# Expert numbers by steps, one-hots with pairs, modulation spread evenly, three projections by block

## The chip, the cores and the metric

One core of one Trainium2 chip runs the whole program. The metric is the device time of one execution in microseconds (us).

## The reference, cut to what matters

Two layers, each a mixer (HGRN2 and S5 branches, a merge and an output projection) and a PEER layer: a search for 16 of 16384 single-neuron experts per token and head, by two sets of 128 keys. The expert search is what the change rewrites:

```python
s = einsum('thpd,hpnd->thpn', q, keys)            # 8 heads, 2 halves, 128 keys
s1_v, s1_i = top_k(s[:, :, 0, :], 16)
s2_v, s2_i = top_k(s[:, :, 1, :], 16)
cand_v = s1_v[..., :, None] + s2_v[..., None, :]          # 16 x 16 sums
cand_i = s1_i[..., :, None] * 128 + s2_i[..., None, :]    # their expert numbers
top_v, top_j = top_k(cand_v, 16)
idx = take_along_axis(cand_i, top_j)
gate = softmax(top_v)
act = gelu(einsum('thkd,td->thk', u_tab[idx], h))
out = einsum('thk,thkd->td', gate * act, v_tab[idx])
```

The mixer starts with `mod = silu(c) @ ada_w[l] + ada_b[l]`, 48 vectors of 128 per layer, which scale, shift and gate the blocks of features.

## The kernel before

Everything is kept by blocks of 128 features (8) and 512 tokens. A dense matrix product is three matmuls per block, since both sides are split into a high and a low part (`whi`/`wlo` by ScalarE and VectorE, L114 and L116; the inputs are `ahi`/`alo`). Weights come in pieces of 128x1024 floats (512 KB), tile `raw`, four buffers, on SyncE's queue.

**Mixer.** Projections, eight heads, then gates, GLU and output projection. A modulation vector is one 128x1024 load, tile `ada`, and one multiply with a row sum on VectorE (L165). Between the gate projections, the GLU and the output products the code calls `later(n)`: 1 vector behind each of 8 projections, 3 ahead of each of 8 GLU products, 4 ahead of four output products.

**Expert stage.** 512 tokens are four blocks of 128. The last block's experts are gathered row by row with indirect DMAs (128 steps for U, L946 on VectorE; 128 for V, L957, tile `gr`, accumulator `gacc`). For the other 384 tokens the kernel computes all 16384 products of U: `dense_U`, 128 times 24 matmuls of 128x384, evicted as `uo` (L788) and written out to `sA`. The gates become a dense matrix by one-hot matmuls. `select(tb)` finds the experts of a token block: 16 best of 50 candidates per head by VectorE's maximum instructions, then, for each of 128 places, L855 compares a row of 50 counters with the found place and sums the candidates' expert numbers (tile `jk`). `build(tb, sel, g8)` makes for four tokens the one-hots of the two key numbers on VectorE (`P` L900, `Qo` L902), multiplies the second by the gate's high and low halves (`Q`, two times L906), and TensorE multiplies the pairs, eight f16 matmuls of 128x128 (L912, L913, tile `pa`). In `P` and `Q` the four tokens lie innermost, so that each matmul reads every fourth element. There are 96 builds per layer; the code puts one `dense_U` and one gather step behind every second. ScalarE evicts `pa` into `stg`, and 48 tokens at a time go out to `sW`.

**Value stage.** For each of 128 pieces of V, `A` (from `sA`) times `W` (from `sW`) on VectorE (L1007), a split into `gh`/`gl`, and 24 matmuls (L1020 to L1022) into eight accumulators that take all of PSUM.

The framework's scheduler orders each engine's instructions by priority and its own estimate of times, so the order within an engine is fixed when the program is built.

Of the kernel before, what the change touches and what calls it, by code (L numbers as in the profile page):

```python
# [4 lines left out]
F32 = mybir.dt.float32  # L5
# [11 lines left out]
T = 512  # L17
# [24 lines left out]
def trunk(tc, a, dbg=None, layers=L, n_i2=128):  # L42
# [17 lines left out]
    def ptile(shape, tag):  # L60
        return psp.tile(shape, F32, tag=tag, name=nm(tag), bufs=PB[tag])
# [420 lines left out]
    def mixer(l, h):  # L482
# [13 lines left out]
        G.memset(toe, 0.0)  # L496
        s5_maps(l, sm, fx, hp, ("w1", "w2", "w3"))
        pk0 = pack_tile(fx)
        dcol = fx.tile([128, 32], F32, name=nm("dcol"))
        for j in range(4):  # L500
            nc.sync.dma_start(dcol[32 * j:32 * j + 32, :], a["dsk"][l])
# [230 lines left out]
        gates(J - 2, fx)  # L732
# [5 lines left out]
        def later(n, l_=l, todo=todo):  # L738
            n = min(n, len(todo))
            if n:  # L740
                ada(l_, [todo.pop(0) for _ in range(n)], hp, "ada")

        for e in range(J):
            ps = proj(40 + e)
            sg = hp.tile([128, T], F32, tag="F", name=nm("sg"))
            S.activation(sg, ps, AF.Sigmoid)
            V.tensor_tensor(yap[:, e, :], yap[:, e, :], sg, op=OP.mult)
            later(1)
        ysf = fx.tile([128, J, T], F32, name=f"ysf{l}")
        ya = []  # L750
        for u in range(J):
# [6 lines left out]
        dump(f"ys{l}", ysf)  # L758
        mg = []
        for e in range(J):  # L760
            later(3)
            ps = dense(a["glu"][l, e], ya)
            sg = hp.tile([128, T], F32, tag="F", name=nm("sg"))
            S.activation(sg, ps, AF.Sigmoid, bias=vec["glub"][:, l, e:e + 1])
            V.tensor_tensor(sg, sg, sgb[e], op=OP.mult)
            V.tensor_tensor(yap[:, e, :], sg, yap[:, e, :], op=OP.add)
# [5 lines left out]
                                   op0=OP.mult, op1=OP.add)  # L772

        for e in range(J - 3):
            later(4, l + 1, follow)
# [22 lines left out]
    def peer(l, h, rows, gp):  # L798
# [13 lines left out]
        def scores(p, ps):  # L812
# [9 lines left out]
            for tb in range(NB):  # L822
                wk = rp.tile([128, 128], F32, tag="wk", name=nm("wk"))
                top16(sv[:, tb, p], sx[:, tb, p], s[:, tb], wk)

        def select(tb):
            val = sv[:, tb].rearrange("p (h s) k -> p h s k", s=2)
            idf = rp.tile([128, 16, 16], F32, tag="idf", name=nm("idf"), bufs=1)
            V.tensor_copy(idf, sx[:, tb])
            idv = idf[:].rearrange("p (h s) k -> p h s k", s=2)  # L830
            V.tensor_scalar(idv[:, :, 0, :], idv[:, :, 0, :], 128.0, None, op0=OP.mult)
            cv = rp.tile([128, 8, NCAND], F32, tag="cv", name=nm("cv"), bufs=1)
            ci = rp.tile([128, 8, NCAND], F32, tag="ci", name=nm("ci"), bufs=1)
            for src, dst in ((val, cv), (idv, ci)):
                for r in range(5):
                    n = CAND[r]
                    V.tensor_tensor(dst[:, :, COFF[r]:COFF[r] + n], src[:, :, 0, r:r + 1].to_broadcast([128, 8, n]),
                                    src[:, :, 1, 0:n], op=OP.add)
                V.tensor_tensor(dst[:, :, COFF[5]:COFF[8]].rearrange("p h (r b) -> p h r b", b=2),
                                src[:, :, 0, 5:8, None].to_broadcast([128, 8, 3, 2]),  # L840
                                src[:, :, 1, None, 0:2].to_broadcast([128, 8, 3, 2]), op=OP.add)
                V.tensor_tensor(dst[:, :, COFF[8]:], src[:, :, 0, 8:16],
                                src[:, :, 1, 0:1].to_broadcast([128, 8, 8]), op=OP.add)
            tv = rp.tile([128, 8, 16], F32, tag="tv", name=nm("tv"), bufs=1)
            tj = rp.tile([128, 8, 16], U32, tag="tj", name=nm("tj"), bufs=1)
            for hh in range(8):
                wk = rp.tile([128, NCAND], F32, tag="wk2", name=nm("wk2"))
                top16(tv[:, hh], tj[:, hh], cv[:, hh], wk)
            tf = rp.tile([128, 8, 16], F32, tag="tf", name=nm("tf"), bufs=1)
            V.tensor_copy(tf, tj)  # L850
            code = rp.tile([128, 8, 16], F32, tag="code", name=nm("code"), bufs=1)
# [5 lines left out]
            cint = rp.tile([128, 128], I32, tag="cint", name=nm("cint"), bufs=1)  # L857
            V.tensor_copy(cint, code[:].rearrange("p h k -> p (h k)"))
            ii = rp.tile([128, 2, 128], I32, tag="ii", name=nm("ii"), bufs=1)
            V.tensor_scalar(ii[:, 0], cint, 7, None, op0=OP.logical_shift_right)  # L860
            V.tensor_scalar(ii[:, 1], cint, 127, None, op0=OP.bitwise_and)
            fx = rp.tile([128, 3, 128], F32, tag="fx", name=nm("fx"), bufs=1)
            V.tensor_copy(fx[:, 0:2], ii)
# [15 lines left out]
            gh = rp.tile([128, 2, 128], F16, tag="gh", name=nm("gh"))  # L879
            V.tensor_copy(gh[:, 0], pt[:, 2])  # L880
            V.tensor_tensor(gh[:, 1], pt[:, 2], gh[:, 0], op=OP.subtract)
            return st, gh

        stg = {}
# [1 line left out]
        def build(tb, sel, g8):  # L886
# [7 lines left out]
            sh = [128, 128, NT]  # L894

            def row(t):
                return t[:, None, :].to_broadcast(sh)
# [5 lines left out]
            Qs = []  # L903
            for i in range(2):
                q = rp.tile(sh, F16, tag=f"Q{i}", name=nm("Q"))
                V.tensor_tensor(q, Q_, row(gh[:, i, c]), op=OP.mult)  # L906
                Qs.append(q)
            for b in range(NT // 4):
                ps = ptile([128, 4, 128], "pa")
                for k in range(4):  # L910
                    t = 4 * b + k
                    TE.matmul(ps[:, k], P_[:, :, t], Qs[0][:, :, t], start=True, stop=False)  # L912
                    TE.matmul(ps[:, k], P_[:, :, t], Qs[1][:, :, t], start=False, stop=True)  # L913
# [285 lines left out]
```

## Time and profile before

| | us |
|---|---|
| median of 3 runs | 3928.33 (3924.42 to 3931.42) |
| the profiled execution, its own time | 3930.45 |
| its span, first to last instruction | 3928.7 |
| TensorE busy in the span | 3736.3 (95%) |
| VectorE busy | 3238.6 (82%) |
| ScalarE busy | 1574.6 (40%) |
| GpSimd busy | 1021.7 (26%) |
| mean granted TensorE clock | 0.97 |

The profiled execution lies 0.05% above the median. Busy shares are means over stages: mixer, expert stage and value stage of each layer have different limits, so the stages are to be read apart.

### The profile page before, as it was taken

To read this page: it belongs to the slowest core of one execution; us is meant where nothing else is said; L and a number is where in the kernel's file an instruction comes from. 1 tells how busy PE (TensorE), PEld (TensorE's weight loads), DVE (VectorE), ACT (ScalarE), POOL (GpSimd) and SP (SyncE) were. 2 spreads that over 40 slices of the span, in tenths; PEclk is the share of its full clock that TensorE was granted. 3 is DMA by queue.
4 is the path that set the end of the run, shared out by engine and by line. 5 is a ranking of instruction groups with operands and counts; after the bars stand their busy time and mean duration, and the time that the engine had idled before them with its cause. 6 is when DMAs were issued, how large, how long until landed. Compare 5 with 4: busy or idle time off the path is not lost.

```text
span 3928.7 us, 62542 instructions
## 1 busy us (share of the span) xinstructions
PE 3736.3 (95%) x21878; PEld 3502.1 (89%) x21878; DVE 3238.6 (82%) x8715; ACT 1574.6 (40%) x2507; POOL 1021.7 (26%) x1475
## 2 busy tenths in 40 slices
PE   6999999999999959999999999999999997699998
PEld 5888878999999959999988887789999997699998
DVE  6998787999898879877578886679998888787874
ACT  3554443333343323333345554344333433233332
POOL 7454100013222344221033440000232223432210
PEclk9999999999999969999999999999999998899999
DMA  5222384379998989998622225524898898999984
GB/s 197 74 64 78 102 266 143 111 249 318 326 315 304 322 300 351 348 344 315 208 85 75 71 81 168 187 84 136 303 309 315 310 325 289 333 353 344 347 294 134
DMA packets 368764, 911.37 MB, mean 232 GB/s; under 512 B 35824, under 2 KB 187440, under 8 KB 368448
## 3 DMA queue, kind: packets, MB, share of 16 engines
q1 hardware_dynamic: 247696, 536.56, 40.6%
q0 software_dynamic: 73952, 268.56, 19.7%
q10 hardware_dynamic: 46800, 102.26, 6.8%
q8 instruction: 172, 2.82, 0.3%
q14 instruction: 144, 1.18, 0.1%
HBM read 796.09 MB, written 111.15 MB: 231 GB/s over the span
## 4 chain that ended last, share of the span: by engine, by line
PE 77%; DVE 11%; DMA 7%; POOL 2%; issue 2%; ACT 1%; SPq 0%; ACTq 0%; DVEq 0%; POOLq 0%
PE mm L132 12%; PE mm L133 12%; PE mm L134 12%; PE mm L1021 3%; PE mm L1020 3%; PE mm L1022 3%; PE pb L1021 2%; PE pa L1022 2%; PE pb L1020 2%; PE pa L1021 2%; PE pa L1020 2%; PE pb L1022 2%; DMA ada<-ada 2%; DVE wlo L116 2%; PE pa L912 2%; PE pa L913 2%
## 5 line engine op out<-in xcount | busy, mean ns | idle before, releaser
L114 ACT ACTIVATE whi<-raw 128x1024 fp32r<-128x1024 f32 x688 | 728.4, 1060 | 1289.0 <-PE mm L133 751.2
L133 PE MATMUL mm<-alo,whi 128*128 128x384 f32 (+1 forms) x3360 | 1217.2, 363 | 13.6 <-DVE alo L123 13.5
L134 PE MATMUL mm<-ahi,wlo 128*128 128x384 f32 (+1 forms) x3360 | 1216.7, 363 | 10.5 <-DVE wlo L116 10.4
L132 PE MATMUL mm<-ahi,whi 128*128 128x384 f32 (+1 forms) x3360 | 1216.7, 364 | 10.5 <-ACT ahi L229 3.5
L116 DVE TENSOR_TENSOR wlo<-raw,whi 128x1024 fp32r<-128x1024 f32 x688 | 842.1, 1225 | 319.6 <-ACT whi L114 299.5
L133 PEld LDWEIGHTS mm<-alo,whi 128*128 128x128 f32 x3360 | 638.0, 190 | 63.7 <-DVE alo L123 14.8
L134 PEld LDWEIGHTS mm<-ahi,wlo 128*128 128x128 f32 x3360 | 638.1, 190 | 62.6 <-DVE wlo L116 14.0
L132 PEld LDWEIGHTS mm<-ahi,whi 128*128 128x128 f32 x3360 | 638.5, 190 | 61.6 <-ACT ahi L229 4.6
L936 POOL DMA_INDIRECT gr<-ur,idi x256 | 269.5, 1053 | 1481.4 <-DVE jk L855 764.6
L936 POOL DMA_INDIRECT gr<-v,idi x256 | 350.6, 1370 | 669.1 <-DVE gacc L957 583.0
L957 DVE SCALAR_TENSOR_TENSOR gacc<-gr,gate,gacc 128x1024 f32<-128x1024 f32 x254 | 324.5, 1277 | 45.3 <-DMA gr<-v,idi 45.0
L946 DVE SCALAR_TENSOR_TENSOR gr<-gr,rows 128x1024 f32<-128x1024 f32 x256 | 311.1, 1217 | 25.9 <-DMA gr<-ur,idi 24.2
L1021 PE MATMUL mm<-gl,whi 128*128 128x384 f32 x768 | 259.0, 338 | 0.7 <-DVE gl L1011 0.6
L1022 PE MATMUL mm<-gh,wlo 128*128 128x384 f32 x768 | 258.5, 337 | 0.0
L1020 PE MATMUL mm<-gh,whi 128*128 128x384 f32 x768 | 210.0, 338 | 50.6 <-ACT gh L1009 26.4
L1009 ACT ACTIVATE gh<-A 128x384 fp32r<-128x384 f32 x256 | 132.4, 518 | 296.7 <-DVE A L1007 257.8
L912 PE MATMUL pa<-Q,P 128*128 128x128 f16 x768 | 197.7, 296 | 45.2 <-DVE Q L906 42.9
L855 DVE SCALAR_TENSOR_TENSOR jk<-iof,tf,ci 128x50 f32<-128x50 f32 x1024 | 223.8, 262 | 0.0
L914 ACT ACTIVATE stg<-pa 128x512 f32<-128x512 f32 x192 | 114.0, 598 | 220.4 <-PE pa L913 192.2
L913 PE MATMUL pa<-Q,P 128*128 128x128 f16 x768 | 187.9, 295 | 0.9
L1020 PEld LDWEIGHTS mm<-gh,whi 128*128 128x128 f32 x768 | 140.6, 189 | 51.2 <-ACT gh L1009 51.2
L1020 PE MATMUL pb<-gh,whi 128*128 128x384 f32 x512 | 172.8, 338 | 0.0
(382 smaller groups left out, 6642.9 us busy)
## 6 DMA issues: line engine op xcount, KB each, us to landing
raw<-u SPq DMA_DIRECT2D x256, 512.0 KB
raw<-v SPq DMA_DIRECT2D x256, 512.0 KB
raw<-win SPq DMA_DIRECT2D x112, 512.0 KB
ada<-ada SPq DMA_DIRECT2D x96, 512.0 KB
sA<-uo ACTq DMA_DIRECT2D x256, 192.0 KB
sW<-stg ACTq DMA_DIRECT2D x64, 768.0 KB
A<-sA SPq DMA_DIRECT2D x256, 192.0 KB
W<-sW SPq DMA_DIRECT2D x64, 768.0 KB
```

The source lines that it names most:

```text
L114: S.activation(hi, raw, AF.Copy)
L116: V.tensor_tensor(lo, raw, hi[:].bitcast(F32), op=OP.subtract)
L132: TE.matmul(ps, hi[:, w], ah, start=(j == 0), stop=False)
L133: TE.matmul(ps, hi[:, w], al, start=False, stop=False)
L134: TE.matmul(ps, lo[:, w], ah, start=False, stop=(j == J - 1))
L912: TE.matmul(ps[:, k], P_[:, :, t], Qs[0][:, :, t], start=True, stop=False)
L936: G.indirect_dma_start(out=g[:], out_offset=None, in_=tab, in_offset=bass.IndirectOffsetOnAxis(ap=ids[:, s_:s_ + 1], axis=0))
L946: V.scalar_tensor_tensor(g, g, 1.0, rows, op0=OP.mult, op1=OP.mult, accum_out=dot[:, s_:s_ + 1])
L957: V.scalar_tensor_tensor(acc_, g, gate[:, s_:s_ + 1], acc_, op0=OP.mult, op1=OP.add)
L1020: TE.matmul(ps, w[0][:, c], g[0], start=first, stop=False)
L1021: TE.matmul(ps, w[0][:, c], g[1], start=False, stop=False)
L1022: TE.matmul(ps, w[1][:, c], g[0], start=False, stop=last)
```

## The change

Four edits. In `select`, the expert number of a found place is no longer looked up among 50 candidates: `ranks` compares the place with 15 thresholds at once, adds up the differences between successive first-key numbers for the thresholds passed, and picks the second key among 16 by its rank, for half the heads at a time, in f16. In `build` both one-hots are made by one instruction, with the key numbers stored twice side by side, and each token's one-hot lies contiguous. The modulation vectors are spread evenly over 27 places from the gate projections to the output products, and those of the next layer join the list. The first layer's first three projections, whose weights are loaded at the start, are written as one loop over blocks of features.

```diff
+    thr = cst.tile([128, 15, 2], F16, name="thr")
...
+    def rank_tables():
+        V.tensor_copy(rnk, iof[:, 0:16, None].to_broadcast([128, 16, 2]))
+        for r in range(1, 16):
+            G.memset(thr[:, r - 1], float(COFF[r]))
+            G.memset(cnd[:, r - 1], float(CAND[r - 1]))
...
+            for j in range(J):
+                ah, al = h[j]
+                w = slice(128 * j, 128 * j + 128)
+                for i, (hi, lo) in zip(order, ws):
+                    TE.matmul(opened[i], hi[:, w], ah, start=(j == 0), stop=False)
+                    TE.matmul(opened[i], hi[:, w], al, start=False, stop=False)
+                    TE.matmul(opened[i], lo[:, w], ah, start=False, stop=(j == J - 1))
...
-        todo = list(range(16, 48))
-        follow = list(range(16)) if l + 1 < layers else []
+        todo = [(l, i) for i in range(16, 48)] + [(l + 1, i) for i in range(16) if l + 1 < layers]
+        parts = 6 + 8 + 8 + 5
+        share = [len(todo) * (k + 1) // parts - len(todo) * k // parts for k in range(parts)]
...
+        def ranks(iv, j, o0, o1):
+            j = j.rearrange("p h k -> p (h k)")
...
+            def total(w, n, o):
+                while n > 2:
+                    m = (n + 1) // 2
+                    V.tensor_tensor(w[:, 0:n - m], w[:, 0:n - m], w[:, m:n], op=OP.add)
+                    n = m
+                V.tensor_tensor(o, w[:, 0], w[:, 1], op=OP.add)
...
+            ge, w = work(15), work(15)
+            V.tensor_tensor(twos(ge), twos(j[:, None].to_broadcast([128, 15, 64])), pairs(thr, 15), op=OP.is_ge)
+            V.tensor_tensor(twos(w), twos(ge), pairs(cnd, 15), op=OP.mult)
+            r2 = rp.tile([128, 64], F16, tag="r2", name=nm("r2"), bufs=1)
+            total(w, 15, r2)
+            V.tensor_tensor(r2, j, r2, op=OP.subtract)
+            gate_rows(ge, step, 15)
+            total(ge, 15, o0)
+            o0 = o0.rearrange("p (h k) -> p h k", h=4)
+            V.tensor_tensor(o0, o0, iv[:, :, 0, 0:1].to_broadcast([128, 4, 16]), op=OP.add)
+            eq = work(16)
+            V.tensor_tensor(twos(eq), twos(r2[:, None].to_broadcast([128, 16, 64])), pairs(rnk, 16), op=OP.is_equal)
+            gate_rows(eq, second, 16)
+            total(eq, 16, o1)
...
-            for hh in range(8):
-                for k in range(16):
-                    jk = rp.tile([128, NCAND], F32, tag="jk", name=nm("jk"))
-                    V.scalar_tensor_tensor(jk, iof[:, 0:NCAND], tf[:, hh, k:k + 1], ci[:, hh], op0=OP.is_equal,
-                                           op1=OP.mult, accum_out=code[:, hh, k:k + 1])
...
-            st = rp.tile([128, 2, 128], F16, tag="slot", name=nm("slot"))
-            S.activation(st, pt[:, 0:2], AF.Copy)
...
+            st = rp.tile([128, 128, 2, 2], F16, tag="slot", name=nm("slot"), bufs=1)
+            gh = rp.tile([128, 128, 2, 2], F16, tag="gh", name=nm("gh"), bufs=1)
...
-            P_ = rp.tile(sh, F16, tag="P", name=nm("P"))
-            V.tensor_tensor(P_, io4, row(st[:, 0, c]), op=OP.is_equal)
-            Q_ = rp.tile(sh, F16, tag="Qo", name=nm("Qo"))
-            V.tensor_tensor(Q_, io4, row(st[:, 1, c]), op=OP.is_equal)
...
+            PQ = rp.tile([128, NT, 2, 128], F16, tag="PQ", name=nm("PQ"))
+            V.tensor_tensor(PQ[:].rearrange("p t i (a b) -> p (t i) a b", b=2), ioh[:, None].to_broadcast(sh), pairs(st),
+                            op=OP.is_equal)
...
-                    TE.matmul(ps[:, k], P_[:, :, t], Qs[0][:, :, t], start=True, stop=False)
+                    TE.matmul(ps[:, k], PQ[:, t, 0], QQ[:, t, 0], start=True, stop=False)
```

Where the instructions now stand. On TensorE, before, at the end of layer 0's expert stage (P and Q are the one-hots, the `mm` of L1020 is the first value accumulator), the last build ran straight into the value matmuls:

```order
L912 LDWEIGHTS P_12614
L912 MATMUL pa_12622<-Q_12618,P_12614 128x128
L913 LDWEIGHTS P_12614
L913 MATMUL pa_12622<-Q_12620,P_12614 128x128
L1020 MATMUL mm_15647<-gh_15666,whi_15657 128x384
L1020 MATMUL mm_15648<-gh_15666,whi_15657 128x384
L1020 MATMUL mm_15649<-gh_15666,whi_15657 128x384
```

In the changed kernel the last build of that layer (PQ, QQ) is followed by `dense_U` (`mm<-ahi,whi`):

```order
L982 LDWEIGHTS PQ_11522
L982 MATMUL pa_11527<-QQ_11524,PQ_11522 128x128
L983 LDWEIGHTS PQ_11522
L983 MATMUL pa_11527<-QQ_11524,PQ_11522 128x128
L142 MATMUL mm_13919<-ahi_6422,whi_13915 128x384
L143 MATMUL mm_13919<-alo_6423,whi_13915 128x384
L144 MATMUL mm_13919<-ahi_6422,wlo_13917 128x384
```

and the value matmuls (now L1090) follow on the last `dense_U`, 17 of them later:

```order
L143 MATMUL mm_14511<-alo_6435,whi_14507 128x384
L144 MATMUL mm_14511<-ahi_6434,wlo_14509 128x384
L142 MATMUL mm_14511<-ahi_6436,whi_14507 128x384
L143 MATMUL mm_14511<-alo_6437,whi_14507 128x384
L144 MATMUL mm_14511<-ahi_6436,wlo_14509 128x384
L1090 MATMUL mm_14552<-gh_14571,whi_14562 128x384
L1090 MATMUL mm_14553<-gh_14571,whi_14562 128x384
```

So 23 builds, counted on TensorE, that stood behind the last `dense_U` now stand before it. On VectorE, before, near the end of one look-up (`jk` into `code`, then the shifts that part the two keys, and the next block's candidate numbers `ci`):

```order
L116 TENSOR_TENSOR wlo_10220<-raw_10216,whi_10218 128x1024
L855 SCALAR_TENSOR_TENSOR jk_8045,code_7794<-iof,tf_7792,ci_7727 128x50
L855 SCALAR_TENSOR_TENSOR jk_8047,code_7794<-iof,tf_7792,ci_7727 128x50
L855 SCALAR_TENSOR_TENSOR jk_8049,code_7794<-iof,tf_7792,ci_7727 128x50
L858 CAST cint_8051<-code_7794 128x128
L837 TENSOR_TENSOR ci_8068<-idf_8064 128x8x16
L837 TENSOR_TENSOR ci_8068<-idf_8064 128x8x8
L837 TENSOR_TENSOR ci_8068<-idf_8064 128x8x5
L837 TENSOR_TENSOR ci_8068<-idf_8064 128x8x4
L860 TENSOR_SCALAR ii_8053<-cint_8051 128x128
L861 TENSOR_SCALAR ii_8053<-cint_8051 128x128
```

In the changed kernel, inside one `ranks` (`s` holds the comparisons, 960 = 15 x 64, halved by the sums; `gr` is a gather step):

```order
L126 TENSOR_TENSOR wlo_10189<-raw_10185,whi_10187 128x1024
L892 TENSOR_TENSOR s_9205<-s_9204,cnd 128x960
L874 TENSOR_TENSOR s_9205<-s_9205 128x448
L881 TENSOR_TENSOR s_9204<-s_9204,step_9200 128x960
L1016 SCALAR_TENSOR_TENSOR gr_9473,dot_8118<-gr_9473,rows_6421 128x1024
L874 TENSOR_TENSOR s_9205<-s_9205 128x256
L934 TENSOR_TENSOR fx_9199<-tv_9147 128x128
L126 TENSOR_TENSOR wlo_10257<-raw_10253,whi_10255 128x1024
L874 TENSOR_TENSOR s_9204<-s_9204 128x448
```

The 128 look-ups of a token block have become 40 longer instructions between the same splits and gather steps. The first step of the gathers stands behind 18 `dense_U` splits in layer 0 instead of 22, and 20 `gacc` steps instead of 26 stand before the first value product.

## Rows read from the trace of the kernel before

**Rows 1.** The page: busy time by engine, and the chain that ended last.
```profile
PE 3736.3 (95%) x21878; PEld 3502.1 (89%) x21878; DVE 3238.6 (82%) x8715; ACT 1574.6 (40%) x2507; POOL 1021.7 (26%) x1475
...
PE 77%; DVE 11%; DMA 7%; POOL 2%; issue 2%; ACT 1%; SPq 0%; ACTq 0%; DVEq 0%; POOLq 0%
```

**Rows 2.** Windows: each engine's busy us (instructions), granted clock, DMA share, GB/s.
```profile
757.00:840.00 83.00, 83.00 (x484) 83.00 (x483) 81.91 (x581) 35.52 (x50) 3.02 (x3) 1.00 0.56 171
840.00:1347.00 507.00, 504.74 (x3063) 490.24 (x3063) 460.68 (x1552) 198.12 (x291) 139.18 (x131) 1.00 0.91 318
1347.00:1436.00 89.00, 42.48 (x285) 35.15 (x283) 68.92 (x135) 21.66 (x37) 43.18 (x24) 0.61 0.83 292
1436.00:1860.00 424.00, 423.29 (x2394) 422.65 (x2394) 354.10 (x575) 153.33 (x199) 129.26 (x98) 0.99 0.95 341
2692.00:3373.00 681.00, 627.71 (x3817) 604.65 (x3815) 609.08 (x2255) 253.06 (x371) 179.25 (x158) 0.95 0.85 297
```

**Rows 3.** TensorE's waits, 757 to 1436 us: total, times, longest.
```profile
PE mm L1020 <- DMA s5s<-ldt: 24.2, 1, 24.2
PE pa L912 <- DVE Q L906: 20.8, 10, 7.0
```

**Rows 4.** The eviction of one candidate block, 757 to 1436 us: ns min/median/max, first, last.
```profile
L788 ACT ACTIVATE uo<-mm x128: 465/471/498, 757.1 to 1364.7; 128x384 f32<-128x384 f32 x128
```

**Rows 5.** Timeline of TensorE in that stage: start, us, line, names.
```profile
1060.21 0.33 PE L132 MATMUL mm<-ahi,whi 128*128 128x384 f32 x1
...
1063.33 0.33 PE L132 MATMUL mm<-ahi,whi 128*128 128x384 f32 x1
...
1063.68 0.29 PE L912 MATMUL pa<-Q,P 128*128 128x128 f16 x1
...
1064.75 0.43 PE L132 MATMUL mm<-ahi,whi 128*128 128x384 f32 x1
```

**Rows 6.** Timeline of TensorE in the first mixer, whole-width and 128-wide matmuls.
```profile
45.64 0.39 PE L134 MATMUL mm<-ahi,wlo 128*128 128x512 f32 x1
...
46.55 0.40 PE L134 MATMUL mm<-ahi,wlo 128*128 128x512 f32 x1
...
82.79 1.05 PE L627 MATMUL pa<-Q,K 128*128 128x128 f32 x8
...
83.68 1.06 PE L672 MATMUL pa<-R 128*128 128x128 f32 x8
```

**Rows 7.** VectorE's lines, 757 to 1436 us: count, busy us, mean ns, idle before.
```profile
L116 DVE TENSOR_TENSOR wlo<-raw,whi 128x1024 fp32r<-128x1024 f32 x128 | 156.3, 1221 | 26.0 <-ACT whi L114 25.5
...
L906 DVE TENSOR_TENSOR Q<-Qo,gh 128x512 f16<-128x512 f16 x192 | 73.0, 417 | 5.1 <-PE pa L912 5.1
...
L900 DVE TENSOR_TENSOR P<-io,slot 128x512 f16<-128x512 f16 x96 | 39.5, 416 | 5.8 <-PE pa L913 5.7
...
L1007 DVE TENSOR_TENSOR A<-A,W 128x384 f32<-128x384 f32 x2 | 1.0, 554 | 1.6 <-DMA W<-sW 1.6
```

**Rows 8.** Windows of the look-up's instructions alone (tile jk).
```profile
757.00:1436.00 679.00, 113.65 (x1024) 0.95 0.86 296
```

**Rows 9.** Timeline of the first hand-over to the value matmuls, all engines.
```profile
1427.45 0.33 SPq L1035 DMA_DIRECT2D A<-sA  x1
...
1427.83 0.43 SPq L1005 DMA_DIRECT2D W<-sW  x1
...
1434.45 1.03 DVE L1007 TENSOR_TENSOR A<-A,W 128x384 f32<-128x384 f32 x2 [1.63 <-DMA W<-sW]
...
1435.62 0.69 PE L1020 MATMUL mm<-gh,whi 128*128 128x384 f32 x1 [24.19 <-DMA s5s<-ldt]
```

**Rows 10.** TensorE's waits, 500 to 600 us and 2400 to 2540 us.
```profile
PE mm L133 <- DVE alo L123: 6.9, 2, 6.4
...
PE mm L133 <- DVE alo L123: 6.7, 1, 6.7
```

**Rows 11.** Timeline of GpSimd before the first layer's small S5 tables.
```profile
22.18 1.15 POOL L286 TENSOR_TENSOR s5s<-s5s 128x32 f32<-128x32 f32 x1 [15.16 <-DMA s5s<-are]
```

More of the change, by code (lines that the diff above doesn't have):

```diff
@@ L488, in mixer @@
         hp = hctx.enter_context(tc.tile_pool(name=f"hp{l}", bufs=2))
+        opened = {}
+        if l == 0:
+            order = list(pre)
+            ws = [pre.pop(i) for i in order]
+            for i in order:
+                opened[i] = ptile([128, T], "mm")
+            for j in range(J):
[5 more added lines that the diff above has]
+                    TE.matmul(opened[i], lo[:, w], ah, start=False, stop=(j == J - 1))
         def proj(i):
+            if i in opened:
+                return opened.pop(i)
             return dense(a["win"][l, i], h, w=pre.pop(i, None) if l == 0 else None)
@@ L498, in mixer @@
         pk0 = pack_tile(fx)
+        if l == 0:
+            rank_tables()
         dcol = fx.tile([128, 32], F32, name=nm("dcol"))
@@ L730, in mixer, with later @@
         hp = mctx.enter_context(tc.tile_pool(name=f"gp{l}", bufs=2))
-        gates(J - 2, fx)
         if l > 0:
             cond(fx, stp)
-        todo = list(range(16, 48))
-        follow = list(range(16)) if l + 1 < layers else []
[L738 to L741, printed above, removed]
+        todo = [(l, i) for i in range(16, 48)] + [(l + 1, i) for i in range(16) if l + 1 < layers]
+        parts = 6 + 8 + 8 + 5
+        share = [len(todo) * (k + 1) // parts - len(todo) * k // parts for k in range(parts)]
+        def later():
+            for _ in range(share.pop(0)):
+                l_, i = todo.pop(0)
+                ada(l_, [i], hp, "ada")
+        for _ in range(J - 2):
+            gates(1, fx)
+            later()
         for e in range(J):
@@ L760, in mixer @@
         for e in range(J):
-            later(3)
+            later()
             ps = dense(a["glu"][l, e], ya)
@@ L774, in mixer @@
         for e in range(J - 3):
-            later(4, l + 1, follow)
+            later()
             merge(e, dense(a["wout"][l, e], mg))
@@ L824, in scores, with work, pairs, twos @@
                 top16(sv[:, tb, p], sx[:, tb, p], s[:, tb], wk)
+        def ranks(iv, j, o0, o1):
+            j = j.rearrange("p h k -> p (h k)")
+            def work(n):
+                return rp.tile([128, T], F32, tag="s", name=nm("s"))[:].bitcast(F16)[:, 0:64 * n].rearrange(
+                    "p (r x) -> p r x", r=n)
+            def pairs(t, n):
+                return t[:, :, None, :].to_broadcast([128, n, 32, 2])
+            def twos(w):
+                return w.rearrange("p r (a b) -> p r a b", b=2)
+            def total(w, n, o):
[4 more added lines that the diff above has]
+                V.tensor_tensor(o, w[:, 0], w[:, 1], op=OP.add)
+            def gate_rows(w, t, n):
+                sh = [128, n * 4, 8, 2]
+                v = w.rearrange("p r (h a b) -> p (r h) a b", h=4, b=2)
+                V.tensor_tensor(v, v, t[:].rearrange("p r h b -> p (r h) b")[:, :, None, :].to_broadcast(sh), op=OP.mult)
+            step = rp.tile([128, 15, 4, 2], F16, tag="step", name=nm("step"), bufs=1)
+            two = [128, 4, 15, 2]
+            V.tensor_tensor(step[:].rearrange("p r h b -> p h r b"), iv[:, :, 0, 1:16, None].to_broadcast(two),
+                            iv[:, :, 0, 0:15, None].to_broadcast(two), op=OP.subtract)
+            second = rp.tile([128, 16, 4, 2], F16, tag="second", name=nm("second"), bufs=1)
+            S.activation(second[:].rearrange("p r h b -> p h r b"), iv[:, :, 1, :, None].to_broadcast([128, 4, 16, 2]),
+                         AF.Copy)
+            ge, w = work(15), work(15)
[12 more added lines that the diff above has]
+            total(eq, 16, o1)
@@ L834, in select @@
-            for src, dst in ((val, cv), (idv, ci)):
+            for src, dst in ((val, cv),):
                 for r in range(5):
@@ L848, in select @@
                 top16(tv[:, hh], tj[:, hh], cv[:, hh], wk)
-            tf = rp.tile([128, 8, 16], F32, tag="tf", name=nm("tf"), bufs=1)
-            V.tensor_copy(tf, tj)
-            code = rp.tile([128, 8, 16], F32, tag="code", name=nm("code"), bufs=1)
-            for hh in range(8):
-                for k in range(16):
-                    jk = rp.tile([128, NCAND], F32, tag="jk", name=nm("jk"))
-                    V.scalar_tensor_tensor(jk, iof[:, 0:NCAND], tf[:, hh, k:k + 1], ci[:, hh], op0=OP.is_equal,
-                                           op1=OP.mult, accum_out=code[:, hh, k:k + 1])
[L857 to L861, printed above, removed]
+            jf = rp.tile([128, 8, 16], F16, tag="jf", name=nm("jf"), bufs=1)
+            V.tensor_copy(jf, tj)
             fx = rp.tile([128, 3, 128], F32, tag="fx", name=nm("fx"), bufs=1)
-            V.tensor_copy(fx[:, 0:2], ii)
+            for hf in range(2):
+                ranks(idv[:, 4 * hf:4 * hf + 4], jf[:, 4 * hf:4 * hf + 4], fx[:, 0, 64 * hf:64 * hf + 64],
+                      fx[:, 1, 64 * hf:64 * hf + 64])
             gv = fx[:, 2].rearrange("p (h k) -> p h k", h=8)
@@ L876, in select @@
                 TE.transpose(pt[:, i], fx[:, i], ident)
-            st = rp.tile([128, 2, 128], F16, tag="slot", name=nm("slot"))
-            S.activation(st, pt[:, 0:2], AF.Copy)
-            gh = rp.tile([128, 2, 128], F16, tag="gh", name=nm("gh"))
-            V.tensor_copy(gh[:, 0], pt[:, 2])
-            V.tensor_tensor(gh[:, 1], pt[:, 2], gh[:, 0], op=OP.subtract)
+            st = rp.tile([128, 128, 2, 2], F16, tag="slot", name=nm("slot"), bufs=1)
+            gh = rp.tile([128, 128, 2, 2], F16, tag="gh", name=nm("gh"), bufs=1)
+            for i in range(2):
+                S.activation(st[:, :, i], pt[:, i, :, None].to_broadcast([128, 128, 2]), AF.Copy)
+            g2 = pt[:, 2, :, None].to_broadcast([128, 128, 2])
+            V.tensor_copy(gh[:, :, 0], g2)
+            V.tensor_tensor(gh[:, :, 1], g2, gh[:, :, 0], op=OP.subtract)
             return st, gh
@@ L911, in build @@
                     t = 4 * b + k
-                    TE.matmul(ps[:, k], P_[:, :, t], Qs[0][:, :, t], start=True, stop=False)
-                    TE.matmul(ps[:, k], P_[:, :, t], Qs[1][:, :, t], start=False, stop=True)
+                    TE.matmul(ps[:, k], PQ[:, t, 0], QQ[:, t, 0], start=True, stop=False)
+                    TE.matmul(ps[:, k], PQ[:, t, 0], QQ[:, t, 1], start=False, stop=True)
                 S.activation(stg[0][:, :, o + 4 * b:o + 4 * b + 4], ps[:].rearrange("p t i -> p i t"), AF.Copy,
```

26 lines of the change are left out of this document (13 added, 13 removed).

## Prediction

> **What bounds the kernel now.** I read the page first: TensorE is busy 95% of the span and makes 77% of the chain that ended last [rows 1]. A mean over stages does not say what a change in one stage is worth, so next I cut the expert stage out by windows [rows 2]. From 757 to 1347 us TensorE is busy all but 2 us, VectorE 542.6 of 590 us. From 1347 to 1436 us TensorE is busy 42 of 89 us at a mean granted clock of 0.61, between its two levels, while VectorE works 69 us. Layer 1 does the same in 681 us (2692 to 3373). So the stage is filled by TensorE and then has a tail in which TensorE waits. The waits say for what [rows 3]: 20.8 us in ten waits for `Q`, the one-hots of a build, and 24.2 us ahead of the first value matmul. The profile puts that last one down to a small load of the S5 tables; the timeline of the hand-over shows the real chain: `A` and `W` loads issued at 1427.45 and 1427.83, their product at 1434.45, whose wait `W` ended, first matmul at 1435.62 [rows 9]. `W` reads `sW`, which the last builds fill. The `dense_U` evictions end at 1364.7 [rows 4]: the value stage starts 71 us after the last of them, because VectorE was behind with the builds.
>
> **What one `dense_U` and one build cost TensorE.** From 1060.21 to 1063.33 stand 18 matmuls: 0.1733 us each, 4.16 us for the 24 of a `dense_U`. From 1063.68 to 1064.75 stand the eight matmuls of a build and one of 0.173 us: 0.90 us a build, 0.112 a matmul [rows 5]. From the first eviction at 757.1 on, the stage holds 127 x 4.16 = 528 us of `dense_U` and 96 x 0.90 = 86 us of builds, 614 us, against 678.5 us that pass up to 1435.6. The other 64 us are the waits and the half clock around them.
>
> **VectorE in the same stretch.** Its windows add to 81.9 + 460.7 + 68.9 = 611.5 us [rows 2]. To price instructions that the trace lacks, I take two lines from rows 7: f32 with 384 elements takes 0.554 us and with 1024 takes 1.221 us, so about 1.04 ns an element and 0.15 us fixed; f16 with 512 takes 0.417 us, so 0.525 ns an element over the same 0.15. The steps:
>
> - The look-up goes: 113.7 us a layer [rows 8]. With it go 48 small instructions (candidate numbers, casts, shifts, 12 for each of four token blocks), at the fixed part and some 50 ns each about 10 us.
> - `ranks` comes: per half of the heads 20 instructions over 7928 elements (three comparisons and products of 960, two of 1024, 960 again for the steps, three summing trees, small rest). At the f16 rate 20 x 0.15 + 7928 x 0.525 ns = 7.2 us, at the f32 rate 11.3; eight halves a layer: 57 us, bound 90.
> - A build: one instruction of 1024 at 0.69 us for two of 0.417, saving 0.15 us, 14 us over 96. The two products stay at 512 elements.
>
> 611.5 - 113.7 - 10 + 57 - 14 = 531 us, and some 7 less for the six accumulations that move behind the hand-over: 524 us. Below 600 us of stage that is about 87% busy, about what VectorE had while TensorE was full. So the 23 builds behind the last `dense_U` fit in, as the order of the new program also has them, and with 17 `dense_U` (71 us) behind the last build the write of `sW` is hidden.
>
> **What one build costs TensorE now.** This is the price that the trace lacks: f16 matmuls with contiguous operands. Upper bound: no change, 0.112 us; contiguous f32 ones of 128x128 also follow each other at 0.89 / 8 = 0.111 us [rows 6]. Lower bound: whole-width matmuls come every 0.91 / 4 = 0.2275 us for 512 columns [rows 6] and every 0.1733 for 384, so 0.054 us per 128 columns and 0.065 us for a matmul of 128. I take 0.080, nearer the lower end, because the new operands have half the bytes of the f32 ones and no stride: 96 x 8 x 0.080 = 61 us; the ends are 50 and 86.
> The Trainium skill, TensorE: Matmul & The Clock Gate, gives in Back-to-back issue gap about 81 ns for a stream of weight load and 128-column matmul; by it the term would be an estimated 62 us. [...]
>
> **The hand-over.** With `sW` long written, the chain of rows 9 still stands: the last `A` and `W` loads sit on SyncE's queue behind a `raw` of V whose buffer comes free when a split behind the last `dense_U` is done, one `L116` of 1.22 us [rows 7]. 1.2 + (1435.62 - 1427.45) = 9.4 us from the last `dense_U` to the first value matmul. If the loads are slower beside the gathers it is 15; if they get ahead it is near nothing.
>
> **DMA.** The stage moves 83 x 171 + 507 x 318 + 89 x 292 = 201 MB (GB/s times us) [rows 2]. Six gathers of 0.52 MB move out: 198 MB. The most that a long stretch has held is 341 GB/s at a share of 0.95, from 1436 to 1860 us [rows 2]. The gathers begin 4 `dense_U` (17 us) earlier, so 66 us at 171 GB/s carry 11 MB and the other 187 MB take 548 us: 614 us. At the page's best slices, some 350 GB/s, it would be 600. So DMA is as long as TensorE: 528 + 61 + 9.4 = 599 us. Two limits this near each other wait for each other now and then; I take 611 us.
>
> **The other edits.** The waits for `alo` at the GLU's start [rows 10] may shrink, as fewer `ada` loads stand before them; the order of the splits there hardly moves. I take 5 us for both layers together (bounds 0 and 13, the two waits of 6.4 and 6.7). The 44 additional bias adds on VectorE lie beside projections. The first three projections already ran interleaved block by block in the old order, so 0 (at most 2 us). The 30 small fills on GpSimd stand where it idles 15.16 us [rows 11]; without that cover, at a tenth of a us each, 3 us. `slot` and `gh` have one buffer instead of two: their writers wait for the last build of the block before, and behind ScalarE's write stand weight splits and evictions; at most 2 us at each of four places, taken as 0 because the new order puts it between builds.
>
> **Sum.** Per layer 678.5 - 611 = 67 us, two layers 134, the rest 5: 3930.45 - 139 = 3791, so 3790 us. That is against the profiled execution, which lies 2 us over the median of the runs, within what repeats differ.
>
> **Rivals.**
>
> 1. *The weight load sets the pace however it lies* (0.112 stays). For it: f32 ones without stride run at the same 0.111; against it: those have twice the bytes. TensorE 528 + 86 + 9.4 = 623 us, 55 a layer, 5 for the rest: 3815 us, 3805 to 3830. Chance 0.2.
> 2. *DMA holds only the 318 GB/s of the stage now* [rows 2]. For it: more small writes and gathers in less time; against it: the value stage held 341. 66 us and 187 MB / 0.318 = 588 make 654 us, 25 a layer: 3875 us. Chance 0.1.
> 3. *Everything at its lower bound*: 0.065 a matmul, 350 GB/s, hand-over hidden: about 595 us, 84 a layer, 13 for the modulation: 3750 us. Chance 0.1.
> 4. *The pairs run at the f32 rate, slower than before.* The new comparisons repeat two elements, the old ones four; if f16 in twos is not taken at the f16 rate, a build costs 1.22 + 2 x 0.69 us instead of 1.67, 0.92 more, 88 us for 96 where 14 were saved, and `ranks` 33 more: 524 + 135 = 659 us. The kernel is slower as soon as VectorE has over the 611 us of before; at today's share of the stage (611 / 678.5) it would be 731 us, 53 more a layer: 4035 us. Against it: the rows show runs of four at the f16 rate. The Trainium skill, Vector Engine (DVE) Microarchitecture Reference, 5.1 Performance modes, asks for 2-byte types, unit step and more than one element in the innermost dimension, which twos meet; the runs of four here agree at 0.417 us, and no row shows twos. Chance 0.05.
>
> **How the numbers follow.** The forecast has 0.55, with 3770 to 3810 of its own. The range takes in rivals 1 and 3 and leaves out 2 and 4 with 0.15: 3745 to 3840 us. 0.2% (8 us) is about what a measurement of this kernel can tell from no change. All cases but the fourth are faster by more: faster 0.94, the same 0.01, slower 0.05.
>
> **What would show it.** Right: no build behind the last `dense_U`, waits for the one-hots near zero, first value matmul near 1368 us in layer 0 (757 + 611), PQ near 0.69 and QQ near 0.42 us, eight build matmuls in about 0.64 us, DMA over 320 GB/s from 840 us on. Wrong: TensorE waiting for `wlo` (L126 now) inside the stage, which would be gathers that come late in VectorE's fixed order; PQ over 1 us; value matmuls that wait for `gh` again; or a value stage longer than now because the gathers moved into it.

## The result

The changed kernel takes 3858.74 us (median of 4 runs, 3855.02 to 3862.04) where the kernel before took 3929.36: a ratio of 0.9822, with a 95% interval of 0.9805 to 0.9839. It is faster, as forecast, but by 70.6 us (1.8%) where 139 were forecast; the time lies 19 us above the range.

The page of the changed kernel, its span and its engines' busy time:

```profile
span 3855.5 us, 60666 instructions
PE 3667.9 (95%) x21878; PEld 3434.7 (89%) x21878; DVE 3113.1 (81%) x6744; ACT 1577.5 (41%) x2529; POOL 1046.5 (27%) x1505
```

The shares are within a point of those before [rows 1]; they say nothing about the stages. The windows of the first expert stage and of the value stage behind it, columns as in [rows 2]:

```profile
757.00:840.00 83.00, 83.00 (x483) 83.00 (x482) 80.24 (x381) 36.77 (x54) 10.88 (x10) 1.00 0.63 215
840.00:1375.00 535.00, 507.79 (x3328) 486.91 (x3327) 447.07 (x854) 216.57 (x329) 168.40 (x135) 0.98 0.91 324
1375.00:1398.00 23.00, 3.44 (x20) 3.12 (x19) 12.53 (x17) 2.48 (x5) 9.61 (x8) 0.69 0.98 335
1398.00:1820.00 422.00, 418.91 (x2362) 417.95 (x2363) 352.72 (x574) 150.79 (x197) 135.74 (x105) 0.99 0.95 342
```

The stage begins at 757.3 us as before (757.1), and its first value matmul stands at 1398.1 instead of 1435.6: 37.5 us gained where 67 were forecast. The tail, in which TensorE mostly stands and the granted clock falls (0.61 before, 0.69 now), has shrunk from 89 us to 23, but between 840 and 1375 us TensorE now stands still for 27 us, where it missed 2 of 507 before. Layer 1 gains 40 us (643 us from first eviction to first value matmul, 683 before). From the first value matmul of layer 0 to the first eviction of layer 1, value stage and second mixer, it is 1254.7 us in both kernels. The last value stage is 4 us longer. 37.5 + 40 - 4 = 73.5, against a difference of the two spans of 73.2.

TensorE's waits between 757 and 1400 us, as in [rows 3]:

```profile
PE mm L1090 <- ACT gh L1079: 19.7, 1, 19.7
PE mm L142 <- ACT uo L820: 19.5, 6, 6.7
PE pa L982 <- DVE QQ L974: 4.1, 1, 4.1
PE pc L944 <- DVE fx L899: 2.7, 1, 2.7
PE mm L144 <- DVE wlo L126: 0.8, 2, 0.6
```

The waits for the one-hots are down from 20.8 us to 4.1. The wait ahead of the first value matmul, at the hand-over from the expert stage to the value stage, is 19.7 us where it was 24.2. New are 19.5 us in six waits of a `dense_U` for an eviction `uo`, of which the kernel before had a single one in the whole program, of 0.3 us. The chain of waits around the longest of these, and ScalarE's timeline of the same place:

```profile
1304.58 0.50 ACT uo L820 x2
1305.08 17.14 DMA sA<-uo
1322.24 0.50 ACT uo L820
1322.78 0.69 PE mm L142
1323.47 0.32 PE mm L143
```

```profile
1300.35 3.14 ACTq L988 DMA_DIRECT2D sW<-stg  x4
1304.58 0.85 ACT L820 ACTIVATE uo<-mm 128x384 f32<-128x384 f32 x2
1305.08 1.75 ACTq L821 DMA_DIRECT2D sA<-uo  x2
1322.24 0.49 ACT L820 ACTIVATE uo<-mm 128x384 f32<-128x384 f32 x1 [5.28 <-DMA sA<-uo]
```

ScalarE issues four transfers of 48 finished tokens to `sW` (768 KB each, 3.1 MB together), then the writes of the two `uo` buffers. The first of these needs 17 us to land where the median of the stage is 4.8. Until then there is no free `uo`, so no accumulator of a `dense_U` is emptied, and TensorE waits 6.74 us. It goes on at 0.32 us a matmul instead of 0.173, at the lower of the two clock levels (mean granted clock 0.83 from 1317 to 1337 us). The chain at the hand-over:

```profile
1378.33 0.94 issue
1379.27 0.48 ACT uo L820
1379.77 5.92 DMA sA<-uo
1385.77 0.33 SPq L1105
1386.15 0.43 SPq L1075
...
1396.95 0.56 DVE A L1077
1397.53 0.53 ACT gh L1079
1398.11 1.33 PE mm L1090 x3
```

The first `A` load is issued 0.08 us after the last `uo` write has landed. What stands between it and the product is put down by the profile to the small S5 tables again. `W`, issued at 1386.15, lands 7.6 us later, at 1393.8; but in VectorE's order an accumulation `gacc` stands ahead of the product and waits 5.07 us for its rows, until 1395.75, so the product starts at 1396.95.

What VectorE and TensorE now pay, VectorE's lines from 757 to 1398 us and TensorE's timeline of one build:

```profile
L974 DVE TENSOR_TENSOR QQ<-PQ,gh 128x512 f16<-128x512 f16 x192 | 71.5, 421 | 0.1
L970 DVE TENSOR_TENSOR PQ<-ioh,slot 128x1024 f16<-128x1024 f16 x96 | 64.0, 685 | 20.5 <-PE pa L983 20.3
L1027 DVE SCALAR_TENSOR_TENSOR gacc<-gr,gate,gacc 128x1024 f32<-128x1024 f32 x20 | 25.6, 1282 | 19.3 <-DMA gr<-v,idi 19.2
L901 DVE TENSOR_TENSOR s<-r,rnk 128x1024 f16<-128x1024 f16 x8 | 5.5, 682 | 0.0
```

```profile
1050.81 0.34 PE L142 MATMUL mm<-ahi,whi 128*128 128x384 f32 x1
1050.98 0.23 PE L982 MATMUL pa<-QQ,PQ 128*128 128x128 f16 x1
1051.02 0.42 PE L143 MATMUL mm<-alo,whi 128*128 128x384 f32 x1
1051.29 0.23 PE L983 MATMUL pa<-QQ,PQ 128*128 128x128 f16 x1
1051.35 0.22 PE L982 MATMUL pa<-QQ,PQ 128*128 128x128 f16 x1
...
1051.63 0.22 PE L983 MATMUL pa<-QQ,PQ 128*128 128x128 f16 x1
1051.66 0.42 PE L144 MATMUL mm<-ahi,wlo 128*128 128x384 f32 x1
1051.92 0.34 PE L142 MATMUL mm<-ahi,whi 128*128 128x384 f32 x1
```

The build's matmuls come every 0.057 us instead of 0.112. From 1050.98 to 1051.92 stand eight of them and two of `dense_U`: 0.94 - 2 x 0.173 = 0.59 us a build, 0.90 before.

### The profile page after: what moved, and what is told of

Same layout as the page of the kernel before. It is cut to its first block, busy times and chain, and to the rows that moved or that the text cites. A ratio compares the mean times of both kernels' runs of the same rounds, so it can differ in the third digit from the quotient of the medians.

```text
span 3855.5 us, 60666 instructions
## 1 busy us (share of the span) xinstructions
PE 3667.9 (95%) x21878; PEld 3434.7 (89%) x21878; DVE 3113.1 (81%) x6744; ACT 1577.5 (41%) x2529; POOL 1046.5 (27%) x1505
## 3 DMA queue, kind: packets, MB, share of 16 engines
q0 software_dynamic: 73952, 268.56, 19.5%
## 4 chain that ended last, share of the span: by engine, by line
PE 72%; DMA 11%; DVE 8%; issue 3%; ACT 2%; POOL 2%; ACTq 1%; SPq 0%; DVEq 0%; POOLq 0%
PE mm L142 11%; PE mm L143 11%; PE mm L144 11%; DMA sA<-uo 5%; PE mm L1090 4%; PE mm L1091 4%; PE mm L1092 3%; PE pa L1092 2%; PE pb L1092 2%; PE pa L1091 2%; PE pb L1091 2%; PE pa L1090 2%; PE pb L1090 2%; DMA gr<-ur,idi 2%; DMA ada<-ada 2%
## 5 line engine op out<-in xcount | busy, mean ns | idle before, releaser
L143 PE MATMUL mm<-alo,whi 128*128 128x384 f32 (+1 forms) x3336 | 1213.0, 364 | 10.4 <-DVE alo L133 10.4
L1006 POOL DMA_INDIRECT gr<-ur,idi x256 | 316.6, 1237 | 1416.8 <-DMA sA<-uo 724.9
L1006 POOL DMA_INDIRECT gr<-v,idi x256 | 328.8, 1284 | 678.0 <-DVE gacc L1027 576.6
L1090 PE MATMUL mm<-gh,whi 128*128 128x384 f32 x768 | 215.1, 339 | 41.6 <-ACT gh L1079 41.6
L1090 PEld LDWEIGHTS mm<-gh,whi 128*128 128x128 f32 x768 | 140.9, 189 | 43.5 <-ACT gh L1079 43.5
L1090 PE MATMUL pa<-gh,whi 128*128 128x384 f32 x512 | 172.7, 337 | 0.0
L1090 PE MATMUL pb<-gh,whi 128*128 128x384 f32 x512 | 172.7, 337 | 0.0
L1092 PE MATMUL pa<-gh,wlo 128*128 128x384 f32 x512 | 172.4, 337 | 0.0
L1092 PE MATMUL pb<-gh,wlo 128*128 128x384 f32 x512 | 172.2, 336 | 0.0
L1091 PE MATMUL pa<-gl,whi 128*128 128x384 f32 x512 | 172.2, 336 | 0.0
## 6 DMA issues: line engine op xcount, KB each, us to landing
sW<-stg ACTq DMA_DIRECT2D x64, 768.0 KB, 12.3
```

Of the source, the lines that this page charges most:

```text
L143: TE.matmul(ps, hi[:, w], al, start=False, stop=False)
L1006: G.indirect_dma_start(out=g[:], out_offset=None, in_=tab, in_offset=bass.IndirectOffsetOnAxis(ap=ids[:, s_:s_ + 1], axis=0))
L1090: TE.matmul(ps, w[0][:, c], g[0], start=first, stop=False)
L1091: TE.matmul(ps, w[0][:, c], g[1], start=False, stop=False)
L1092: TE.matmul(ps, w[1][:, c], g[0], start=False, stop=last)
```

## The experiments

Two questions: which edit brought the 70 us, and where the other half went. On the first, theory V says that VectorE's look-up had made the builds late and that its removal brings most of the gain; rival P says that it is TensorE's cheaper builds. On the second, theory Q says that the stage waits in queues: two `uo` buffers whose writes stand behind `sW`, and a first `A` load that waits for the last `uo`. Rival B says that the stage's bytes are the bound (some 199 MB at 310 GB/s in its 641 us), so that each wait removed comes back elsewhere. Where an edit has no diff here, it is the part of the change that the text names.

**Single edits.** Applied to the kernel before:

> The kernel before with the look-up by steps alone; one-hots, modulation and projections as before. Theory V (VectorE's look-up was what made the builds late): the builds move ahead of the last dense_U, the expert stage keeps 528 + 86 us of TensorE work and some 20 us of waits, 640 to 650 us instead of 679, so 3860 to 3880 us. Rival P (the gain of the change came from TensorE's cheaper builds): no more than 10 us a layer from here, 3905 to 3930 us.

Measured: 3884.69 us, ratio 0.9883 (0.9867 to 0.9898), 45 us. The stages fall to 655 and 653 us. A little less than theory V had, since 16 us of waits for `uo` (0.3 before) and 32 us ahead of value matmuls (51 before) stand here already.

> The kernel before with the one-hots by pairs alone; the look-up as before. Theory V: VectorE keeps 611 - 14 us of work and the builds still end behind the last dense_U, so 5 to 15 us a layer, 3900 to 3920 us. Rival P: TensorE saves 96 x 0.3 = 29 us a layer at once, 3870 us or less. Eight build matmuls near 0.5 us in both.

Measured: 3922.29 us, ratio 0.9982 (0.9972 to 0.9992), 8 us. Rival P falls: TensorE saves its 0.3 us a build and waits instead: 58.5 us for `QQ` in the whole program (42.9 for `Q` before) and 20.5 for `uo` (0.3 before). The two edits alone bring 45 and 8 us, together 70: cheaper builds count only once VectorE delivers them in time.

> The kernel before with the two mixer edits alone (modulation spread evenly, first three projections by block). After the whole change the first eviction of the expert stage stands at 757.3 us against 757.1, so the theory says 0: 3925 to 3933 us. The prediction on record had 5 us for it (rival): 3920 to 3925 us.

Measured: 3927.85 us, ratio 0.9992 (0.9983 to 1.0001): 2 us, and no difference from zero that this can tell; an interval from -7 to 0 does not exclude the 5 us either.

**Stride in the build's matmuls.**

```diff
...
-                    TE.matmul(ps[:, k], PQ[:, t, 0], QQ[:, t, 0], start=True, stop=False)
-                    TE.matmul(ps[:, k], PQ[:, t, 0], QQ[:, t, 1], start=False, stop=True)
+                    TE.matmul(ps[:, k], p4[:, 0, :, t], q4[:, 0, :, t], start=True, stop=False)
+                    TE.matmul(ps[:, k], p4[:, 0, :, t], q4[:, 1, :, t], start=False, stop=True)
```

Here `p4` and `q4` are the same buffers seen as (2, 128, 4).

> The changed kernel, with only the build's matmuls changed: they read every fourth element of the same PQ and QQ buffers, as the kernel before did, so its products are of mixed tokens and the output is not the reference's. VectorE, DMA and all else stay. If stride sets the pace of the build's matmuls, eight take 0.9 us instead of 0.45 to 0.6. Theory Q (TensorE and waits in queues bound the stage): 96 x 0.3 = 29 us a layer come back, 3858 + 45 to 60 = 3903 to 3918 us. Theory B (the bytes of the stage bound it, 199 MB at 310 GB/s): the added TensorE time hides behind transfers, 3858 to 3875 us.

Measured: 3905.53 us, ratio 0.9943 (0.9928 to 0.9959), 47 us more than the changed kernel. A matmul comes every 0.118 us again. TensorE's busy time in the two expert stages rises by 76 us (630 and 634 us, 594 each in the changed kernel), the stages by 48 (664 and 667), as the waits for `uo` fall from 47 us to 13.6. So some three fifths of the longer TensorE work show in the time, where rival B had it hidden: B loses its first test. It is not a clean one, since the order of the program moved with the edit (19 `dense_U` behind the last build, 17 in the changed kernel).

> The changed kernel; of the build's matmuls only the loaded operand PQ is read with a stride of four elements, QQ lies contiguous (products of mixed tokens, output not the reference's). With both strided a matmul came every 0.118 us, with none every 0.057. If the loaded operand's stride sets the pace: 0.118 here, and about 3900 us; if the streamed one does: 0.057, about 3859 us.

Measured: 3867.21 us, ratio 0.984 (0.9817 to 0.9864); a matmul every 0.057 us, though its weight load lasts 113 ns.

> The changed kernel; of the build's matmuls only the streamed operand QQ is read with a stride of four elements, PQ lies contiguous (products of mixed tokens, output not the reference's). The mirror of the run before: 0.118 and about 3900 us if the streamed operand's stride sets the pace, 0.057 and about 3859 us if the loaded one does.

Measured: 3902.79 us, ratio 0.9922 (0.9905 to 0.9938). Its timeline of TensorE:

```profile
1041.35 0.30 PE L985 MATMUL pa<-QQ,PQ 128*128 128x128 f16 x1
1041.47 0.30 PE L984 MATMUL pa<-QQ,PQ 128*128 128x128 f16 x1
1041.58 0.29 PE L985 MATMUL pa<-QQ,PQ 128*128 128x128 f16 x1
```

0.117 us each: the stride of the streamed operand sets the pace, that of the loaded one does not.

**Buffers and queues.** `UB` is the number of `uo` buffers:

```diff
-UB = 2
+UB = 4
```

> The changed kernel with four buffers of uo instead of two. Theory Q: TensorE's waits for uo (19.5 us in layer 0, 27 in layer 1) come from two buffers whose writes to sA stand behind 3.1 MB of sW; with four they go, and the stage shortens by 15 to 25 us a layer: 3810 to 3830 us. Theory B (bytes bound the stage): the wait only moves, to raw or to the gathered rows, 3845 to 3862 us.

Measured: 3782.25 us, ratio 0.9621 (0.9605 to 0.9637): 77 us under the changed kernel, more than either theory said. Windows of its stages and TensorE's waits from 757 to 1400 us:

```profile
840.00:1345.00 505.00, 496.19 (x3299) 475.89 (x3298) 435.17 (x846) 211.76 (x326) 158.63 (x127) 0.99 0.93 334
...
755.40:1366.40 611.00, 587.25 (x3827) 566.63 (x3825) 527.66 (x1241) 253.00 (x385) 177.47 (x143) 0.99 0.89 317
...
2618.40:3225.50 607.10, 585.68 (x3826) 565.63 (x3824) 526.65 (x1236) 252.72 (x386) 178.75 (x143) 0.99 0.89 319
```

```profile
PE mm L1090 <- DMA s5s<-ldt: 14.9, 1, 14.9
PE pa L982 <- DVE QQ L974: 4.6, 2, 4.1
```

The stage takes 611 and 607 us, no wait for `uo` is left, and the transfers run at 334 GB/s where they made 324: B falls. Between the two spans lie 74.3 us: 65.5 in the two expert stages, 4 in the last value stage and 5 in the mixers, which the edit does not touch. Of the 65.5, 47 are the waits for `uo`, 7 the two hand-overs (19.7 and 16.2 to 14.9 and 13.9) and 15 TensorE's busy time (594 to 587 us and 594 to 586; the granted clock of layer 0's stage goes from 0.97 to 0.99); 3 come back in other waits.

> The changed kernel with three buffers of uo. A dense_U and its share of a build take TensorE 4.45 us at least, and a write of uo takes up to 18 us behind sW, so n buffers and the three accumulators in PSUM cover about (n + 3) x 4.5 us from the last free buffer: 22 us with two, 27 with three, 31 with four, against eviction, weight splits and sW's issue that stand before the write. Theory Q: most but not all of the gain of four buffers: 3790 to 3820 us. If the gain of four buffers came from another order of the program and not from depth, no such step shows: 3840 us or more, or the same 3782.

Measured: 3799.08 us, ratio 0.9675 (0.9654 to 0.9696): between two and four buffers, as a matter of depth should be. The program's order moves with the number of buffers, though: 12 `dense_U` stand behind the last build with three and with four, 17 with two. So the step from two buffers to three mixes depth and order, and what ties it to the buffers are the waits for `uo`, which fall from 47 us to 4.4.

```diff
-        nc.scalar.dma_start(sA[l][i], t)
+        nc.sync.dma_start(sA[l][i], t)
```

> The changed kernel with uo written to sA on SyncE's queue instead of ScalarE's, two buffers as before. If the writes are late because they stand behind sW in one queue (theory Q), they land in about 5 us all through and the waits for uo go: 3815 to 3835 us, if SyncE's loads of raw do not suffer. If all queues share the same engines and sW slows every transfer alike (theory B, or a variant of Q), the landing stays up to 17 us and the time 3850 to 3870 us.

Measured: 3817.26 us, ratio 0.9703 (0.9682 to 0.9723). The waits for `uo` fall from 47 us to 8.5, with two buffers as before. The longest landing in layer 0 is 13.9 us where it was 18.4, the median 5.1. The landing times in the traces of both layers, parted by whether an `sW` was in transit when the write was issued, have these medians: with `sW` 16.3 us in the changed kernel, on the same queue, and 10.3 here, on the other; without it 4.6 and 4.7. So both parts hold: the place behind `sW` in the queue, and transfers that slow each other across queues.

```diff
-                dense_U(l, ui[0], h, rp)
+                dense_U(l, ui[0], h, gp)
```

> The changed kernel with uo (two buffers) in the pool that outlives the expert stage, so that the memory of A and W of the value stage is not that of uo. Theory: the first A load waits for the last write of uo because A takes over its memory; then the loads start earlier and the hand-over falls from 19.7 and 16.2 us to 5 to 10: 3830 to 3845 us. Rival: the A load waits for the writes of sA itself or stands behind the raw loads of V: 3850 to 3862 us.

Measured: 3823.57 us, ratio 0.9726 (0.971 to 0.9742). SyncE's timeline and, in a second view, TensorE's at the hand-over:

```profile
1341.23 0.33 SPq L112 DMA_DIRECT2D raw<-u  x1
1341.80 0.90 SPq L1105 DMA_DIRECT2D A<-sA  x1
```

```profile
1379.41 0.33 PE L144 MATMUL mm<-ahi,wlo 128*128 128x384 f32 x1
1379.58 0.34 PE L1090 MATMUL mm<-gh,whi 128*128 128x384 f32 x1
```

The first `A` is loaded 38 us before the last `dense_U` ends, and the first value matmul follows that one without a gap. So it was the memory of `uo` that `A` waited for, not `sA` itself. The waits for `uo` stay (54.5 us), and it gains 35 us all the same.

**Fewer bytes.**

```diff
-                g = gather(a["ur"], iu, s_)
+                if s_ % 2 == 0:
+                    g = gather(a["ur"], iu, s_)
```

> The changed kernel with every second gather of U rows left out (VectorE works on the same rows twice; the output is not the reference's). It takes 33.5 of the stage's 199 MB away and no instruction of TensorE, VectorE or ScalarE. Theory B (bytes at 310 to 324 GB/s bound the stage): the stage falls to TensorE's 594 us and a hand-over, 605 to 615 us: 3790 to 3810 us. Theory Q (queue order and two buffers): sW still lands ahead of uo's writes, only somewhat faster, and the stage loses 5 to 15 us: 3830 to 3850 us.

Measured: 3884.55 us, ratio 0.9892 (0.9875 to 0.9909), slower than the changed kernel and outside both theories. The order of the program had moved with the edit: in each layer 51 accumulations of V now stand ahead of the last one-hots on VectorE (none in the changed kernel) and 14 builds behind the last `dense_U` (none). Why the scheduler chose this order is not shown. Its VectorE line from 757 to 1398 us and its waits of TensorE:

```profile
L1028 DVE SCALAR_TENSOR_TENSOR gacc<-gr,gate,gacc 128x1024 f32<-128x1024 f32 x59 | 75.5, 1279 | 22.8 <-DMA gr<-v,idi 22.8
```

```profile
PE pa L982 <- DVE QQ L974: 15.8, 14, 3.7
```

The hand-over waits 24.7 us: it is the tail of the kernel before over again. As a test of bytes the run is spoiled; it shows that late builds cost more than 33.5 MB less can give back.

**Both mends.** Four buffers of `uo`, in the other pool:

> The changed kernel with both mends: four buffers of uo, in the pool that outlives the expert stage. Theory Q: the two waits are separate, so the gains add; from the 3782 us of four buffers the hand-over of 14.9 and 13.9 us goes nearly whole: 3750 to 3765 us. Rival B (bytes): at 199 MB in 611 us the stage is as fast as transfers allow, and without the hand-over the waits come back elsewhere: 3775 to 3785 us.

Measured: 3757.25 us, ratio 0.9547 (0.953 to 0.9564), where theory Q had it, and 101 us under the changed kernel. Windows of its two expert stages:

```profile
757.80:1363.70 605.90, 589.82 (x3826) 568.09 (x3825) 525.57 (x1276) 252.30 (x385) 167.82 (x137) 0.99 0.89 315
2613.00:3204.60 591.60, 584.75 (x3827) 564.42 (x3826) 520.05 (x1235) 252.23 (x385) 168.52 (x137) 1.00 0.90 321
```

In layer 1 TensorE waits 7 us in 592: the stage is bounded by TensorE.

## Why the prediction was wrong, step by step

- **What bounds the stage: right.** The builds were late for VectorE, and without the look-up none stands behind the last `dense_U`. The single edits bear it out: 45 us for the look-up, 8 for the cheaper builds alone.
- **VectorE's terms: right.** `PQ` 0.685 us (0.69 said), `QQ` 0.421 (0.42), the rank instructions 57 us a layer (57; sum of their lines). In all VectorE is busy 540 us in the changed kernel's stage of 641, and 527.7 in the stage of 611 with four buffers (524 said). The pairs run at the f16 rate: rival 4 falls with the 0.685 us.
- **A build on TensorE: right, a little dear.** 0.59 us against 0.64, 57 us a layer against 61. A matmul alone (0.057) is under the lower bound of 0.065; the two `dense_U` matmuls at the seams, 0.27 and 0.26 instead of 0.173, give more than that back. Rival 1 falls. What my reason for the value named together, half the bytes and no stride, the stride runs take apart: among f16 matmuls it is the streamed operand's stride. Why f32 ones take 0.111 without a stride [rows 6] is not shown.
- **The hand-over: wrong step.** 9.4 us said, 19.7 and 16.2 measured. I kept the chain of [rows 9] and took the `raw` ahead of `A` on SyncE's queue for what releases it. That `raw` was issued in time; `A` waited for the last `uo` write, 5.92 us, as its memory is `uo`'s. Before, the late `sW` had hidden that. So `A` was issued 7.4 us after the last `dense_U` instead of 1.2, and from there to the first matmul it took 12.3 us instead of 8.2, 3 of them because the accumulation stood ahead of the product. "Value matmuls that wait for `gh` again" was among the signs of being wrong, and it came.
- **"Two limits this near each other wait for each other now and then; I take 611 us": the step that failed.** The 12 us are an allowance for which the prediction names no wait. Against them stand 19.5 us of waits for `uo`, 7.6 us of others and 5 us more of TensorE's busy time (594, 589 said). 594.2 + 19.7 + 27.1 = 641.0: of the 30 us over 611, 15 are waits, 10 the hand-over and 5 busy time. The 19.5 us were no meeting of two limits but a queue with two buffers, and the trace of before held the sign, in ScalarE's waits, which I did not read beside TensorE's:

```profile
ACT uo L788 <- DMA sA<-uo: 20.8, 7, 5.7
```

  ScalarE waited 20.8 us for `uo` there already, and TensorE was not held by it (0.3 us). The changed kernel issues `sW` every 48 us instead of 57 (eight groups from 968 to 1302 us, before from 1012 to 1415), and TensorE is back for an accumulator after 4.16 + 2 x 0.59 = 5.3 us instead of 4.16 + 2 x 0.90 = 6.0. Two runs agree with this: with the cheaper builds alone the waits rise from 0.3 us to 20.5, and with strided builds in the changed kernel they fall from 47 us to 13.6; how much the order of the program did in each is not shown.
- **DMA: the 341 GB/s were not needed, and rival 2 was wrong in its reason.** Its 3875 us came nearest to the time, which was luck: with four buffers the same stage runs at 334 GB/s. It moves 194 MB there (611 us x 317) and 199 in the changed kernel, 198 said; with both mends layer 1 takes 592 us, under the 600 to 614 that I had called the DMA's bound.
- **The other edits: 5 us said, 2 measured**, with an interval that holds both 0 and 5. The waits for `alo` went from 13.5 to 10.4 us, and the stage behind them did not start earlier.
- **The sum.** Of the missing 68 us, 56.5 lie in the two expert stages (67 forecast for each, 37.5 and 40 measured), 4 in the last value stage (2.9 of them two waits for `gh`), 5 in the mixers, and 2.6 between the spans profiled and the medians. With four buffers the stages take 611 and 607 us where 611 were forecast, and the kernel 3782, 8 under the forecast. The terms on VectorE and TensorE were right, and the range left out a queue that was already waiting. That the 611 us are met exactly is partly luck: the hand-over is 14.9 us there instead of 9.4, the other waits 9 instead of 12, the busy time 587 instead of 589.

## What to carry to other kernels

When a change takes away the wait that ended last, read the waits of every engine that feeds or empties the one in question, also those that cost nothing now: a buffer that is two deep and already waits is the next bound. Count for each ring of buffers the longest landing of its writes, not the median, and see what else is issued on the same queue in bursts. And where a later stage reuses the memory of an earlier one, the last reader of that memory stands in the chain of the hand-over, whatever the data needs.

## What the runs showed of the hardware

An f16 matmul of 128 columns came every 0.057 us with a contiguous streamed operand and every 0.117 with one of four elements' stride; the stride of the loaded operand made no difference in that pace (0.057). The f32 matmuls of 128x128 at 0.111 [rows 6] are no guide to f16. The Trainium skill, TensorE: Matmul & The Clock Gate, gives in Back-to-back issue gap about 81 ns for such a stream and in LDWEIGHTS (loading the stationary operand) about 107 ns for a load. The loads' rows agree with the second, 98 to 117 ns each (medians); the pace does not follow from it, since one starts every 57 ns and two overlap, and it lies under the first. Here the measurement decides.

A write of 192 KB landed in 4.8 us (median in layer 0), and in up to 18.4 behind a burst of 3.1 MB on the same queue; moved to SyncE's queue, where loads of `raw` stand ahead of it, it took up to 13.9.
